# A two-layer diffusion trunk: the last output pair of layer 0 in another product order, and a conditioning block moved beside the last projection

## The chip, the core and the metric

The kernel runs on one core of a Trainium2 chip. The metric is the device time of one execution in microseconds (us). Three runs of the kernel before took 2236.32, 2233.32 and 2235.29 us; the median is 2235.29.

## The reference

One inference step of a trunk with two layers, width 2048, for 640 tokens: 128 context tokens and 512 latent tokens. All data are float32. A layer is

```python
h = rms_norm(x) * (1 + scale) + shift      # scale, shift, gate from silu(cond) @ ada_w + ada_b
y = mixer(h @ w_in, ...)                   # layer 0: banded attention and a short convolution
                                           # layer 1: differential attention (C) and dense attention (D)
x = x + gate * (y @ w_out)
```

`cond` differs between context and latent tokens, so each channel has two values (two "columns" c) of scale, shift and gate. Layer 1's attention also reads cached keys and values. Outputs are x after layer 1 and the new keys and values.

## The kernel before

**Layout.** Channels lie on the 128 partitions and the 640 tokens on the free axis; x, h and y are 16 tiles of 128x640, numbered k or n. A product of float32 is taken as three matmuls of a hi and a lo part: hi times hi, hi times lo, lo times hi. For that each operand is split: ScalarE (ACT) writes the hi part and VectorE (DVE) subtracts it (lines 329 and 330, function `split`; for weights the tiles are `wh` and `wl`, for activations both are called `h`). A matmul is 128x128 by 128x320, that is one half of the tokens: `HV[0]` is the first half, `HV[1]` the second. The time of the kernel is the PE's stream of these matmuls.

**Stages.** Even input projection, even mixer, output projection of layer 0 (`project_out(0)`), norm of its result, odd input projection ("front", `project`), attention of layer 1 with the rest of the odd columns beside it (`run_tiles`), output projection of layer 1 (`project_out(1)`).

**An output projection** makes three (layer 1: two) leading tiles, then single tiles, then pairs of output tiles. A pair (`run_pairs`) is done with seven products in the manner of Strassen, in the order M1, M5, M6, M2, M7, M3, M4; each product accumulates in one pair of PSUM banks `pq`, and DVE adds it to the residual `xr` (line 1292). M2 completes the first half of the pair's first tile, M7 the second half of its second tile, M3 the second half of its first and M4 the first half of its second (`done`).

**Norm of x1.** After the last pair of layer 0 (tiles 14 and 15), `norm_half` (line 1554) makes the norm of one half of the tokens: the square of the last tile on ACT (1557), sums over the channels as matmuls with a vector of ones (1565), mean and power on DVE and GpSimd (1567 to 1570), a transpose of the result r to a row that all partitions hold (1574), and its copy `rbc` by ACT (1577). `h1_maker` (1593) then makes h of row k: x1 times a scale times rbc on DVE (1611), the shift on ACT (1613), then the split. The x1 tiles come back from memory (`x1_back`), six of them beside the last products (`x1_tail`).

**Conditioning.** scale, shift and gate come in blocks of 512 columns of `ada_w`. For some blocks the product is made on DVE (`ada_rows`, lines 210 to 214): for each of 16 row blocks kt of the weights one load of 256 KB into a tile `adaw`, issued on GpSimd's queue (219), and two DVE instructions of 128x512 that add weight times silu(cond) to a tile `adaS` in PSUM. Block (1, 11) holds layer 1's gates of the output tiles 12 to 15. It runs in the attention stage as `fill1`, a generator from which the loop of `run_tiles` takes steps at the rate `FILL1`; its sums lie in a PSUM buffer of the pool "twice", which the attention scores share.

**Order.** Each engine works in its program order. The order in which the build writes the instructions is set by generators: `prep` (work for the next steps), `attn` (attention and other work beside the projections), `fill` (conditioning). `advance` takes steps from them at fixed places between matmuls, and a `yield` in a generator moves what stands behind it to the next such place. A scheduling pass of the build then orders instructions near one another by their operands. Loads of weights go out on SyncE's queue, stores and the loads of `adaw` on GpSimd's.

**First dense keys.** `keys_first` (1905) splits the first keys of the dense attention; its cached keys `ctxk` are loaded at the start of the attention stage (748) and transposed on PE (757).

The names that the change touches: `run_pairs` (575), `project` and `project_out` (1306, 1350), `x1_last` and `norm_half` (1544, 1554), `h1_maker` (1593), `fill1` (1879), `keys_first` (1905), `score_place` (84).

Of the kernel before, what the change touches and what calls it, by code (L numbers as in the profile page):

```python
# [20 lines left out]
P = 128  # L21
# [29 lines left out]
FILL0_FROM = 6  # L51
FILL1 = 1.15


@with_exitstack
def trunk_kernel(ctx: ExitStack, tc: tile.TileContext, I: dict, O: dict):
# [517 lines left out]

    def run_pairs(cols, w_ap, mov, room, used, begin, done, tail, fill=None, rests=lambda p, name: 0.0):

# [729 lines left out]

    def project(w, cols, n0, maker, job, begin, done, tail, n_lead=3, flip=0, fill=None, rests=lambda p, name: 0.0, **kw):

# [14 lines left out]
        for n in range(n_lead, n0):  # L1323
# [18 lines left out]
            if g is not None:  # L1342
# [3 lines left out]
                  {"B11": half_of(0, 0), "T1": half_of(0, 1), "B21": half_of(8, 0), "B22": half_of(8, 1),  # L1346
                   "T2": form_of(0), "T3": form_of(1), "T4": form_of(2)}, room, used, begin, done, tail, fill, rests)
        drain(prep)

    def project_out(l, maker, finish, last, tail, **kw):  # L1350
# [3 lines left out]
        def job(n):  # L1354
            def f(pp):
                if (l, n) not in loaded:
                    res_load(l, n)
                for i in range(2):
                    res_sum(l, n, pp[i], CS[:1] if i == 0 else CS[1:])
                yield  # L1360
                finish(n)
            return f

        def later(n):
            yield
            finish(n)
# [177 lines left out]
    def x1_last(t, h):  # L1544
        n, sl = KT - 2 + t, HV[h][1]
        if t == h:
            squares(n, sl)
            return
        nc.gpsimd.dma_start(xdram[n], st["xr", n])
        prep.append(norm_half(n, h))  # L1550
        if not h:
            drain(prep)


    def norm_half(n, h):
        sl = HV[h][1]
        A.activation(st["sq"][:, sl], st["xr", n][:, sl], AF.Square)
        yield
# [4 lines left out]
        for i, s in enumerate((st["acc"], st["sq"])):  # L1563
            for b, o in enumerate(starts):
                PE.matmul(tot[:, 4 * i + b:4 * i + b + 1], s[:, o:o + P], ones[:, 0:1], start=True, stop=True)
            if i == 0:
                V.tensor_scalar(ss, tot[:, 0:3], 1.0 / D, EPS, ALU.mult, ALU.add)
            else:
                V.scalar_tensor_tensor(out=ss, in0=tot[:, 4:7], scalar=1.0 / D, in1=ss, op0=ALU.mult, op1=ALU.add)
        G.tensor_tensor(r, ss, half[:, 0:3], op=ALU.pow)  # L1570
# [4 lines left out]
        if h:  # L1575
            st["rbc"] = xr_tile("rbc")
        A.copy(st["rbc"][:, sl], rt[:, 0:HALF])

    x1 = [None] * KT
    BACK = (0, 1, 2, 3, 8, 9, 10, 11, 4, 5, 6, 7, 12, 13)  # L1580
# [9 lines left out]

    project_out(0, y0_maker, x1_done, x1_last, x1_tail, early=early, flip=1)

    def h1_maker(k, hv):
        if k == 0 and hv[0][0]:
            for g in range(3):
# [3 lines left out]
            for i in (14, 15):  # L1599
                x1[i] = st["xr", i]  # L1600
        if k == 12:
            attn.append(forms(hdram))
        if len(hv) == 2 or hv[0][0]:
            new_h(k)
            st["ht", k] = big(f"T{4 + k % 4}")[:, 0:NT]
        t = st["ht", k]
        hi, lo = hs[k]
        toks = TOKS if len(hv) == 2 else (((0, slice(0, HALF), 0, 0),), CS[1:])[hv[0][0]]
        toks = [(x[-3], x[-1]) if len(x) == 4 else x for x in toks]
        for sl, c in toks:  # L1610
            V.scalar_tensor_tensor(out=t[:, sl], in0=x1[k][:, sl], scalar=gsc[1][:, k, c:c + 1],
                                   in1=st["rbc"][:, sl], op0=ALU.mult, op1=ALU.mult)
            A.activation(t[:, sl], t[:, sl], AF.Identity, bias=mod[1][:, k, c:c + 1])
# [258 lines left out]
    st["sets"], st["rp"] = 2, 3  # L1872
    place2, fold2 = (lambda t=t, n=n: pools["cur"].tile([P, NT], F32, tag=t, name="adaw", bufs=n) for t, n in (("x2", 1), ("kk", 2)))

    def scores_twice():
        st["once"] = True
        return pools["twice", "at"]

    fill1 = ada_in_psum([(1, 11)], scores_twice, place2, 1, (fold2, place2), "x2", 1)

# [23 lines left out]
    gated.clear()  # L1904
    def keys_first():
        key_split("k0", *first)
        yield
# [69 lines left out]
    jobs += [(OD["cg"] + i * P, last_gate(i)) for i in (4, 5)]  # L1977
    run_tiles(jobs, I["od_w_in"][0], None, fill1, FILL1, steps=lambda i: 3.3 if i < 5 else 1.85 if i < 13 else 2.6,
              single=lambda i: 0 if i else 2, fill_from=20)
    drain(prep)  # L1980
# [3 lines left out]
    def y1_maker(k):  # L1984
        if k in (6, 7):

            for _ in fill1:
                pass
            drain(attn)
# [40 lines left out]
    def rows_half(n, bs, late):  # L2030
# [4 lines left out]
        for i, b in enumerate(bs):  # L2035
# [62 lines left out]
```

## Time and profile before

| | |
|---|---|
| three runs, median | 2235.29 us (2233.32 to 2236.32) |
| the profiled execution's own time | 2233.99 us |
| its span | 2232.2 us |
| PE busy | 2200.3 us (99%) |
| DVE, ACT, POOL busy | 1745.4, 1137.0, 264.0 us |
| granted TensorE clock, mean | 0.998 |
| output projection of layer 0 ends, odd projection begins | about 1084 to 1091 us |
| odd front | to 1594 us |
| attention with the rest of the odd columns | 1594 to 2012 us |
| output projection of layer 1 | 2012 to 2228 us |

Times in the trace are counted from the start of the span; the profiled execution's own time holds 1.8 us more. Engines are PE (matmul), DVE (VectorE), ACT (ScalarE), POOL (GpSimd) and SP (SyncE). A row of the timeline has start, duration, engine, line of the kernel, operation, and "output<-inputs" by the program's names; in brackets stands how long the engine was idle before it and what ended that. The rows of waits give the sum in us, the number of waits and the longest. The rows of windows give, for a stretch, its length and each engine's busy time with the number of instructions, then the granted clock, the busy share of the DMA engines and GB/s. A matmul's duration (0.31 us) is longer than the distance to the next one, since matmuls are pipelined.

### The profile page before, as it was taken

The numbers are of one execution on the slowest core, as the hardware profiler recorded it, in microseconds if no ns is written. First come the engines' busy times: TensorE is split into PE (matmuls) and PEld (weight loads), VectorE is DVE, ScalarE is ACT, GpSimd is POOL, SyncE is SP. The second block draws the span as 40 slices with busy tenths as digits, with TensorE's granted clock in tenths as the row PEclk, the third lists the DMA queues.
The fourth block names the chain that finished last, engine by engine and source line by source line (L and its number), as shares of the span: only waits on it lengthen the run. The fifth ranks groups of instructions, "written<-read, shape, count | busy, mean of one in ns | idle before, by whom it ended". The sixth has DMA issues, their size and how long they took to land.

```text
span 2232.2 us, 41154 instructions
## 1 busy us (share of the span) xinstructions
PE 2200.3 (99%) x15516; PEld 2125.5 (95%) x15516; DVE 1745.4 (78%) x3047; ACT 1137.0 (51%) x2445; POOL 264.0 (12%) x421
## 2 busy tenths in 40 slices
PE   7999999999999999999999999999999999999999
PEld 5889999999999999999999999999999999999999
DVE  5659898989788977877788878978567687677665
ACT  4335453535334445444654466555578756664343
POOL 3221001000100100000101112211011111111010
PEclk9999999999999999999999999999999999999999
DMA  9985556565454435844675434545532343347541
GB/s 355 341 291 180 168 167 208 181 195 164 146 160 120 146 99 183 249 135 126 226 238 158 148 93 123 175 137 162 170 98 86 96 134 116 102 160 232 162 133 42
DMA packets 380375, 368.47 MB, mean 165 GB/s; under 512 B 18946, under 2 KB 326624, under 8 KB 379664
## 3 DMA queue, kind: packets, MB, share of 16 engines
q1 hardware_dynamic: 357248, 284.78, 42.0%
q0 software_dynamic: 22064, 78.83, 10.1%
q8 instruction: 122, 2.00, 0.4%
q10 hardware_dynamic: 864, 2.23, 0.3%
q14 instruction: 77, 0.63, 0.1%
HBM read 312.41 MB, written 48.11 MB: 162 GB/s over the span
## 4 chain that ended last, share of the span: by engine, by line
PE 90%; DMA 5%; DVE 2%; issue 1%; ACT 1%; POOL 1%; SPq 0%; DVEq 0%; POOLq 0%; ACTq 0%
PE pq L668 13%; PE pq L670 13%; PE pq L669 13%; PE pa L365 6%; PE pa L366 6%; PE pa L367 5%; PE pb L365 5%; PE pb L367 5%; PE pb L366 5%; PE T L908 2%; PE S L920 1%; PE S L922 1%; PE S L921 1%; PE T L698 1%; PE T L196 1%
## 5 line engine op out<-in xcount | busy, mean ns | idle before, releaser
L329 ACT ACTIVATE wh<-raw 128x512 fp32r<-128x512 f32 (+1 forms) x352 | 210.5, 600 | 315.6 <-PE pb L366 188.1
L668 PE MATMUL pq<-h,wh 128*128 128x320 f32 x1152 | 358.2, 311 | 0.0
L669 PE MATMUL pq<-h,wh 128*128 128x320 f32 x1152 | 355.9, 309 | 0.0
L670 PE MATMUL pq<-h,wl 128*128 128x320 f32 x1152 | 355.6, 309 | 0.0
L365 PE MATMUL pa<-h,wh 128*128 128x320 f32 x944 | 299.9, 318 | 0.5 <-DVE gg L1393 0.5
L365 PE MATMUL pb<-h,wh 128*128 128x320 f32 x944 | 296.1, 314 | 0.9 <-ACT h L329 0.9
L366 PE MATMUL pa<-h,wh 128*128 128x320 f32 x944 | 295.0, 313 | 0.4 <-DVE h L330 0.4
L367 PE MATMUL pb<-h,wl 128*128 128x320 f32 x944 | 293.9, 311 | 0.0
L367 PE MATMUL pa<-h,wl 128*128 128x320 f32 x944 | 293.5, 311 | 0.0
L366 PE MATMUL pb<-h,wh 128*128 128x320 f32 x944 | 292.9, 310 | 0.0
L330 DVE TENSOR_TENSOR wl<-raw,wh 128x512 fp32r<-128x512 f32 (+1 forms) x352 | 228.2, 649 | 74.4 <-ACT wh L329 66.7
L668 PE MATMUL pq<-T,wh 128*128 128x320 f32 x864 | 268.8, 311 | 0.0
L670 PE MATMUL pq<-T,wl 128*128 128x320 f32 x864 | 267.1, 309 | 0.0
L669 PE MATMUL pq<-T,wh 128*128 128x320 f32 x864 | 266.9, 309 | 0.0
L329 ACT ACTIVATE wh<-sx 128x512 fp32r<-128x512 f32 x216 | 135.8, 632 | 167.0 <-PE pq L669 110.2
L668 PEld LDWEIGHTS pq<-h,wh 128*128 128x128 f32 x1152 | 216.3, 188 | 1.6 <-issue 1.6
L669 PEld LDWEIGHTS pq<-h,wh 128*128 128x128 f32 x1152 | 216.4, 188 | 0.0
L670 PEld LDWEIGHTS pq<-h,wl 128*128 128x128 f32 x1152 | 216.3, 188 | 0.0
L283 DVE SCALAR_TENSOR_TENSOR acc<-adaw,sT,acc 128x1024 f32<-128x1024 f32 x150 | 189.3, 1276 | 1.3 <-DMA adaw<-in_ada_w 1.3
L365 PEld LDWEIGHTS pa<-h,wh 128*128 128x128 f32 x944 | 177.3, 188 | 12.9 <-issue 11.0
L330 DVE TENSOR_TENSOR wl<-sx,wh 128x512 fp32r<-128x512 f32 x216 | 147.7, 688 | 46.4 <-ACT wh L329 41.7
L366 PEld LDWEIGHTS pa<-h,wh 128*128 128x128 f32 x944 | 177.6, 188 | 4.7 <-issue 4.1
(416 smaller groups left out, 4985.3 us busy)
## 6 DMA issues: line engine op xcount, KB each, us to landing
adaw<-in_ada_w SPq DMA_DIRECT2D x80, 512.0 KB, 4.1
raw<-in_ev_w_in SPq DMA_DIRECT2D x130, 256.0 KB, 3.3
raw<-in_od_w_in SPq DMA_DIRECT2D x112, 256.0 KB, 3.2
w<-in_od_w_in SPq DMA_DIRECT2D x48, 512.0 KB, 4.5
ada<-in_ada_w SPq DMA_DIRECT2D x11, 2048.0 KB, 13.5
adaw<-in_ada_w POOLq DMA_DIRECT2D x75, 256.0 KB, 3.3
w<-in_ev_w_in SPq DMA_DIRECT2D x27, 512.0 KB, 3.8
adah<-in_ada_w SPq DMA_DIRECT2D x20, 512.0 KB, 9.1
```

The lines of the kernel that those rows point to most:

```text
L196: PE.matmul(acc[32 * g:32 * g + 32, 0:wd], sT[:, kt, :], w[:, kt % m, :], start=(i < 4), stop=(i >= KT - 4), tile_position=(0, 32 * g))
L283: V.scalar_tensor_tensor(out=acc[c], in0=w, scalar=sT[:, kt, c:c + 1], in1=acc[c], op0=ALU.mult, op1=ALU.add)
L329: A.activation(hi, x, AF.Copy)
L330: V.tensor_sub(lo, x, hi)
L365: PE.matmul(ps, wh[:, i, :], hi[:, sl], start=(j == js[0] if alone else (pos == 0 and j == 0)), stop=False)
L366: PE.matmul(ps, wh[:, i, :], lo[:, sl], start=False, stop=False)
L367: PE.matmul(ps, wl[:, i, :], hi[:, sl], start=False, stop=(j == js[1] - 1 if alone else (pos == 3 and j == 3)))
L668: PE.matmul(ps, wh[:, j, :], hi, start=(first and h == 0 and j == 0), stop=False, skip_group_check=True)
L669: PE.matmul(ps, wh[:, j, :], lo, start=False, stop=False, skip_group_check=True)
L670: PE.matmul(ps, wl[:, j, :], hi, start=False, stop=(final and h == 1 and j == 3), skip_group_check=True)
L698: PE.transpose(t[:, i * P:(i + 1) * P], src(b), ident)
L908: PE.transpose(t[:, i * P:(i + 1) * P], p, ident)
```

## The change

1. The last pair of layer 0 runs its products in the order M1, M5, M6, M7, M3, M2, M4 (`closing`). With that both second halves (M7, M3) are complete two products before the end. The norm of the second half is given to `prep` beside M2 and M4, the norm of the first half to `attn`, beside the first odd matmuls. `norm_half` takes the row sum of the earlier squares first and the last square behind it, and for the second half it makes h of rows 0 and 1 at once.
2. `h1_maker` multiplies x1 with rbc in one DVE instruction a row and gives the scale to ACT, which applies it with the shift.
3. `keys_first` begins with one more `yield`.
4. Block (1, 11) is taken from attention (`fill1`, `FILL1`, `st["once"]` go) and runs in `project_out(1)` as `fill2`: from single tile 4 on a step per quarter, then in the first pairs, and what is left of it before tile 12's pair begins. Its sums take the score buffer `pS`, its weights one tile `adaw`, later in turn with a third of `tables`. Score tiles of attention now always alternate between two buffers.
5. In layer 1 the residual tiles have four buffers in place of five, and the store of a tile stands one step later.

```diff
-    def run_pairs(..., fill=None, rests=lambda p, name: 0.0):
+    def run_pairs(..., fill=None, rests=lambda p, name: 0.0, closing=None):
...
-        seq = [(p, n) for p in range(len(cols)) for n in MOV]
+        seq = [(p, n) for p in range(len(cols)) for n in (closing if closing and p == len(cols) - 1 else MOV)]
...
     def score_place():
-        if ("twice", "at") not in pools or st.get("once"):
+        if ("twice", "at") not in pools:
...
-        st["xr", n] = pools["cur"].tile([P, NT], F32, tag="xr", name="xr", bufs=5)
+        st["xr", n] = pools["cur"].tile([P, NT], F32, tag="xr", name="xr", bufs=4 if l else 5)
...
                     advance(attn, 1 if len(hv) == 2 else 2)
+                    if n >= fill_at:
+                        next(fill, None)
...
         def begin(p):
             for t in range(2):
                 res_load(l, n0 + 2 * p + t)
+            if l and n0 + 2 * p >= 12:
+                for _ in kw.get("fill") or ():
+                    pass
...
     def x1_last(t, h):
         n, sl = KT - 2 + t, HV[h][1]
-        if t == h:
+        if not h:
+            nc.gpsimd.dma_start(xdram[n], st["xr", n])
+        if h and t:
             squares(n, sl)
-            return
-        nc.gpsimd.dma_start(xdram[n], st["xr", n])
-        prep.append(norm_half(n, h))
-        if not h:
-            drain(prep)
+        elif h:
+            prep.append(norm_half(n, h))
+        elif t:
+            attn.append(norm_half(n, h))
...
+        if not h:
+            squares(n - 1, sl)
+        columns(0, st["acc"])
+        V.tensor_scalar(ss, tot[:, 0:3], 1.0 / D, EPS, ALU.mult, ALU.add)
+        A.activation(st["sq"][:, sl], st["xr", n][:, sl], AF.Square)
+        yield
+        columns(1, st["sq"])
...
         A.copy(st["rbc"][:, sl], rt[:, 0:HALF])
+        if h:
+            for k in range(2):
+                st["ht", k] = xr_tile("ht")
+                h1_maker(k, HV[1:])
...
-        for i in {"M7": range(0, 4), "M3": range(4, 6)}.get(name, ()):
+        for i in {"M7": range(0, 3), "M3": range(3, 6)}.get(name, ()):
...
-        for sl, c in toks:
-            V.scalar_tensor_tensor(out=t[:, sl], in0=x1[k][:, sl], scalar=gsc[1][:, k, c:c + 1],
-                                   in1=st["rbc"][:, sl], op0=ALU.mult, op1=ALU.mult)
-            A.activation(t[:, sl], t[:, sl], AF.Identity, bias=mod[1][:, k, c:c + 1])
+        V.tensor_mul(t[:, sl], x1[k][:, sl], st["rbc"][:, sl])
+        for part, c in toks:
+            A.activation(t[:, part], t[:, part], AF.Identity, scale=gsc[1][:, k, c:c + 1], bias=mod[1][:, k, c:c + 1])
...
+    project_out(0, y0_maker, x1_done, x1_last, x1_tail, early=early, flip=1,
+                closing=("M1", "M5", "M6", "M7", "M3", "M2", "M4"))
...
-    fill1 = ada_in_psum([(1, 11)], scores_twice, place2, 1, (fold2, place2), "x2", 1)
+    fill2 = ada_in_psum([(1, 11)], lambda: pS, place2, 1, (fold2, lambda: tables[:, 2 * 512:3 * 512]), "adaw", 1)
...
     def keys_first():
+        yield
         key_split("k0", *first)
...
+    def fin_rests(p, name):
+        if p == 0 and name == "M1":
+            st["wide"] = [fold2, tables[:, 2 * 512:3 * 512]]
+        return float(name in ("M6", "M2", "M3", "M4"))
...
     project_out(1, y1_maker, rows_out, rows_last, lambda name: None, n_lead=2, order=(0, 2, 3, 1), led=last_pool,
-                lead_pp=(0, 2))
+                lead_pp=(0, 2), fill=fill2, fill_at=4, rests=fin_rests)
```

Lines of the kernel after are lower by one up to about line 1300 and higher by 14 to 31 behind that.

**PE at the border of the layers.** Of before, from the end of M4 (`pq<-T`) over the transposes of r and the column sums (`ones`) to the first odd matmuls (`pb<-h`):

```order
L669 MATMUL pq<-T_10983,wh 128x320
L670 MATMUL pq<-T_10983,wl 128x320
L1574 MATMUL T<-ident,r_12776 128x128 x2
L1574 MATMUL T<-ident,r_12776 128x64
L1565 MATMUL T<-ones,acc 128x1 x3
L1565 MATMUL T<-ones,sq 128x1 x3
L1574 MATMUL T<-ident,r_12809 128x128 x2
L1574 MATMUL T<-ident,r_12809 128x64
L365 MATMUL pb<-h_12858,wh 128x320 x2
L365 MATMUL Sp<-h_12858,wh 128x320
```

Of after, the same end of M4 and what follows:

```order
L668 MATMUL pq<-T_10983,wh 128x320
L669 MATMUL pq<-T_10983,wl 128x320
L1574 MATMUL T<-ones,acc 128x1 x3
L364 MATMUL pb<-h_12779,wh 128x320 x2
L365 MATMUL pb<-h_12779,wh 128x320
L366 MATMUL pb<-h_12779,wl 128x320
L365 MATMUL pb<-h_12779,wh 128x320
L366 MATMUL pb<-h_12779,wl 128x320
L364 MATMUL Sp<-h_12779,wh 128x320
L365 MATMUL Sp<-h_12779,wh 128x320
L364 MATMUL pb<-h_12786,wh 128x320 x2
L1574 MATMUL T<-ones,sq 128x1 x3
```

The transposes and sums no longer stand together: the row of r for the second half (`T<-ident,r_12729`) is now ahead of M4, and behind M4 stand only three column sums before odd matmuls of the second halves begin. The second sums of the first half follow after ten of them, its transposes after six more, and 20 second-half matmuls stand behind those before the first `pa` of a first half.

**PE at the first dense keys.** Of before, in the leading tiles of the attention stage (`Sp<-h`: the product of a lead; one `h` name for each row k):

```order
L365 MATMUL Sp<-h_13135,wh 128x320
L366 MATMUL Sp<-h_13135,wh 128x320
L367 MATMUL Sp<-h_13135,wl 128x320
L757 MATMUL T<-ident,ctxk 128x128 x2
L365 MATMUL Sp<-h_13144,wh 128x320
L366 MATMUL Sp<-h_13144,wh 128x320
L367 MATMUL Sp<-h_13144,wl 128x320
```

Of after:

```order
L364 MATMUL Sp<-h_13133,wh 128x320
L365 MATMUL Sp<-h_13133,wh 128x320
L366 MATMUL Sp<-h_13133,wl 128x320
L364 MATMUL Sp<-h_13141,wh 128x320
L365 MATMUL Sp<-h_13141,wh 128x320
L366 MATMUL Sp<-h_13141,wl 128x320
L756 MATMUL T<-ident,ctxk 128x128 x2
L364 MATMUL Sp<-h_12995,wh 128x320
```

The two transposes of `ctxk` stand behind two more rows of k, that is behind six more matmuls.

**DVE in the final projection.** Of before, from the last single tile's residual to the second product of the first pair (`wl`: lo parts of weights; lines 610 and 619: sums of weights for a product):

```order
L1292 SCALAR_TENSOR_TENSOR xr<-pb,hgt_137,xr 128x192
L1292 SCALAR_TENSOR_TENSOR xr<-pb,hgt_137,xr 128x128
L330 TENSOR_TENSOR wl<-w_25317,wh 128x512 x2
L330 TENSOR_TENSOR wl<-sx,wh 128x512
L1292 SCALAR_TENSOR_TENSOR xr<-pa,hgt_137,xr 128x320
L330 TENSOR_TENSOR wl<-sx,wh 128x512
L610 TENSOR_TENSOR sx<-sx,w_25317 128x1024
L330 TENSOR_TENSOR wl<-sx,wh 128x512 x2
L619 TENSOR_TENSOR sx<-w_25325,sx 128x1024
L330 TENSOR_TENSOR wl<-w_25325,wh 128x512 x2
```

Of after, at the same place:

```order
L1291 SCALAR_TENSOR_TENSOR xr<-pb,hgt_137,xr 128x192
L1291 SCALAR_TENSOR_TENSOR xr<-pb,hgt_137,xr 128x128
L213 SCALAR_TENSOR_TENSOR adaS<-adaw,sT,adaS 128x512
L329 TENSOR_TENSOR wl<-w_25242,wh 128x512
L213 SCALAR_TENSOR_TENSOR adaS<-tables,sT,adaS 128x512 x2
L329 TENSOR_TENSOR wl<-w_25242,wh 128x512
L213 SCALAR_TENSOR_TENSOR adaS<-adaw,sT,adaS 128x512
L329 TENSOR_TENSOR wl<-sx,wh 128x512
L213 SCALAR_TENSOR_TENSOR adaS<-adaw,sT,adaS 128x512
L1291 SCALAR_TENSOR_TENSOR xr<-pa,hgt_137,xr 128x320
L329 TENSOR_TENSOR wl<-sx,wh 128x512
L213 SCALAR_TENSOR_TENSOR adaS<-tables,sT,adaS 128x512
```

Behind the residual, each lo part now has two rows of the conditioning block (`adaS`) around it, on weights that come in turn in `adaw` and in `tables`.

More of the change, by code (lines that the diff above doesn't have):

```diff
@@ L573, in trunk_kernel, with run_pairs @@
     GROUP = {"M1": "M1", "M6": "M1", "M7": "M1", "M4": "M1", "M5": "M5", "M3": "M5", "M2": "M2"}
-    def run_pairs(cols, w_ap, mov, room, used, begin, done, tail, fill=None, rests=lambda p, name: 0.0):
+    def run_pairs(cols, w_ap, mov, room, used, begin, done, tail, fill=None, rests=lambda p, name: 0.0, closing=None):
         ap = pools["cur"]
@@ L1305, in form_of, with project @@
         return lambda j: (T[j][:, 0, i * HALF:(i + 1) * HALF], T[j][:, 1, i * HALF:(i + 1) * HALF])
-    def project(w, cols, n0, maker, job, begin, done, tail, n_lead=3, flip=0, fill=None, rests=lambda p, name: 0.0, **kw):
+    def project(w, cols, n0, maker, job, begin, done, tail, n_lead=3, flip=0, fill=None, rests=lambda p, name: 0.0,
+                closing=None, fill_at=KT, **kw):
         go_on = run_tiles([(cols[n], job(n)) for n in range(n_lead)], w, maker, **{"order": (0, 2, 1, 3), "flip": flip, **kw})
@@ L1346, in project @@
                   {"B11": half_of(0, 0), "T1": half_of(0, 1), "B21": half_of(8, 0), "B22": half_of(8, 1),
-                   "T2": form_of(0), "T3": form_of(1), "T4": form_of(2)}, room, used, begin, done, tail, fill, rests)
+                   "T2": form_of(0), "T3": form_of(1), "T4": form_of(2)}, room, used, begin, done, tail, fill, rests,
+                  closing)
         drain(prep)
@@ L1562, in norm_half, with columns @@
         r = small.tile([P, 3], F32, tag="r", name="r1")
-        for i, s in enumerate((st["acc"], st["sq"])):
+        def columns(i, x):
             for b, o in enumerate(starts):
[L1565 to L1569, printed above, removed]
+                PE.matmul(tot[:, 4 * i + b:4 * i + b + 1], x[:, o:o + P], ones[:, 0:1], start=True, stop=True)
+        if not h:
[3 more added lines that the diff above has]
+        A.activation(st["sq"][:, sl], st["xr", n][:, sl], AF.Square)
+        yield
+        columns(1, st["sq"])
+        V.scalar_tensor_tensor(out=ss, in0=tot[:, 4:7], scalar=1.0 / D, in1=ss, op0=ALU.mult, op1=ALU.add)
         G.tensor_tensor(r, ss, half[:, 0:3], op=ALU.pow)
@@ L1589, in x1_back @@
         nc.sync.dma_start(x1[k], xdram[k])
-    project_out(0, y0_maker, x1_done, x1_last, x1_tail, early=early, flip=1)
     def h1_maker(k, hv):
-        if k == 0 and hv[0][0]:
+        if len(hv) == 1 and k < 2 and hv[0][0] and k in made:
+            return
+        if k == 2 and hv[0][0]:
             for g in range(3):
@@ L1600, in h1_maker @@
                 x1[i] = st["xr", i]
+        if k == 0 and not hv[0][0]:
+            drain(attn)
         if k == 12:
@@ L1603, in h1_maker @@
         if len(hv) == 2 or hv[0][0]:
+            made.add(k)
             new_h(k)
-            st["ht", k] = big(f"T{4 + k % 4}")[:, 0:NT]
+            if k == 2:
+                st["T3"] = big("T3")
+            if k >= 2:
+                st["ht", k] = st["T3"][:, (k - 2) * NT:(k - 1) * NT] if k < 4 else big(f"T{4 + k % 4}")[:, 0:NT]
         t = st["ht", k]
@@ L1872, in trunk_kernel, with place2, fold2 @@
     st["sets"], st["rp"] = 2, 3
[L1873 to L1877, printed above, removed]
-    fill1 = ada_in_psum([(1, 11)], scores_twice, place2, 1, (fold2, place2), "x2", 1)
+    def place2():
+        if not st.get("wide"):
+            return pools["cur"].tile([P, NT], F32, tag="adaw", name="adaw", bufs=1)
+        st["wide"].reverse()
+        return st["wide"][0]() if callable(st["wide"][0]) else st["wide"][0]
+    def fold2():
+        return pools["cur"].tile([P, NT], F32, tag="adaw", name="adaw", bufs=1)
+    fill2 = ada_in_psum([(1, 11)], lambda: pS, place2, 1, (fold2, lambda: tables[:, 2 * 512:3 * 512]), "adaw", 1)
     def key_load(j, tag, bufs):
@@ L1977, in trunk_kernel @@
     jobs += [(OD["cg"] + i * P, last_gate(i)) for i in (4, 5)]
-    run_tiles(jobs, I["od_w_in"][0], None, fill1, FILL1, steps=lambda i: 3.3 if i < 5 else 1.85 if i < 13 else 2.6,
-              single=lambda i: 0 if i else 2, fill_from=20)
+    run_tiles(jobs, I["od_w_in"][0], None, steps=lambda i: 3.3 if i < 5 else 1.85 if i < 13 else 2.6,
+              single=lambda i: 0 if i else 2)
     drain(prep)
```

9 lines of the change are left out of this document (4 added, 5 removed).

## The prediction

> **What bounds the kernel now.** I read the totals first, then the chain that ended last, then the waits of PE summed by what they waited for, and only then single rows at the places where the change acts.
>
> ```profile
> span 2232.2 us, 41154 instructions
> PE 2200.3 (99%) x15516; PEld 2125.5 (95%) x15516; DVE 1745.4 (78%) x3047; ACT 1137.0 (51%) x2445; POOL 264.0 (12%) x421
> PE 90%; DMA 5%; DVE 2%; issue 1%; ACT 1%; POOL 1%; SPq 0%; DVEq 0%; POOLq 0%; ACTq 0%
> ```
>
> PE is busy for 2200.3 of 2232.2 us. The change adds and removes no matmul, so it can only win back PE's waits and slow stretches, or add some. This is what PE waited for behind the start-up (from 40 us on):
>
> ```profile
> PE T L1704 <- DVE on L1699: 1.7, 3, 0.7
> PE T L1574 <- POOL r L1570: 1.6, 2, 1.2
> PE T L757 <- DMA ctxk<-in_cache_d_k: 1.4, 1, 1.4
> PE T L908 <- DVE p L1667: 1.3, 3, 0.6
> PE Sp L365 <- ACT p L889: 1.0, 1, 1.0
> PE pb L365 <- ACT h L329: 0.9, 1, 0.9
> PE T L834 <- DVE ptl L330: 0.8, 3, 0.3
> ...
> PE pa L366 <- DVE h L330: 0.4, 1, 0.4
> ```
>
> The whole list is about 15 us long, so a gain above that is impossible unless a slow stretch goes too. There is one, at the border of the two layers.
>
> **The border of the layers (product order, norm, scale on ScalarE).** PE's rows from the last matmul of product M4 to the first odd matmul, then two odd matmuls one after the other, then the granted clock:
>
> ```profile
> 1083.54 0.30 PE L670 MATMUL pq<-T,wl 128*128 128x320 f32 x1
> 1084.22 0.88 PE L1574 MATMUL T<-ident,r 128*128 128x128 f32 x6 [0.38 <-POOL r L1570]
> 1084.93 0.78 PE L1565 MATMUL T<-ones,acc 128*128 128x1 f32 x6
> 1086.06 0.80 PE L1565 MATMUL T<-ones,sq 128*128 128x1 f32 x6 [0.35 <-ACT sq L1557]
> 1088.10 1.54 PE L1574 MATMUL T<-ident,r 128*128 128x128 f32 x6 [1.24 <-POOL r L1570]
> 1090.53 0.90 PE L365 MATMUL pb<-h,wh 128*128 128x320 f32 x2 [0.88 <-ACT h L329]
> ...
> 1093.10 0.47 PE L366 MATMUL pb<-h,wh 128*128 128x320 f32 x1
> 1093.37 0.47 PE L367 MATMUL pb<-h,wl 128*128 128x320 f32 x1
> ```
> ```profile
> 1083.80:1087.90 4.10, 2.34 (x19) 2.16 (x18) 2.70 (x9) 2.36 (x6) 1.70 (x3) 1.00 0.94 358
> 1087.90:1094.70 6.80, 5.71 (x22) 5.53 (x22) 5.24 (x14) 5.25 (x15) 0.74 (x2) 0.50 0.76 262
> ```
>
> The number 0.50 in the second row is the granted clock. In that stretch 128x320 matmuls start 0.27 us apart (1093.10 to 1093.37), where this kernel otherwise starts them 0.147 us apart (582 matmuls of this and smaller sizes in 84.00 us, in a row quoted below). The loss: from the end of the last slot of M4 (1083.54 + 0.15 = 1083.69) to 1090.53 are 6.84 us; some 15 slow matmuls up to 1094.70 lose 15 x 0.12 = 1.8 us; of these 8.6 us, about 2.0 are work that must be done anyway (two transposes of r at 0.71, the distance of 1084.22 and 1084.93, and two sets of column sums at 0.3). So 6.6 us are lost.
>
> After the change the norm of the second half of the tokens runs beside products M2 and M4, and its h for rows 0 and 1 are ready when M4 ends; the odd projection begins with second halves, and the norm of the first half runs beside them. The chain of that norm is the one of before, whose durations the trace has:
>
> ```profile
> 1087.15 0.90 POOL L1570 TENSOR_TENSOR r<-ss,half 128x3 f32<-128x3 f32 x1 [1.83 <-DVE ss L1569]
> ```
> ```profile
> 1089.68 0.42 ACT L1577 COPY rbc<-T 128x320 f32<-128x320 f32 x1 [1.55 <-PE T L1574]
> 1090.01 0.47 ACT L329 ACTIVATE h<-T 128x320 fp32r<-128x320 f32 x1
> 1090.38 0.73 ACT L1613 ACTIVATE T<-T,mod 128x128 f32<-128x128 f32 x2
> ```
>
> M4 now ends near 1084.75 (the same work, plus a third of a microsecond for a wait on the row sum in M2). The residual of the last tile takes 0.55 us on DVE, its square 0.47 on ACT, the sums 0.16 on DVE, the power 0.90 on POOL. With what stands queued between them on DVE and ACT (the second halves of rows 2 and 3), r is there near 1088.9, while PE reaches its transpose, in program order, after 16 matmuls, near 1088.3: a wait of 0.6 us. Then 20 more second-half matmuls (3 us) cover the copy of rbc (0.42) and the first halves of rows 0 to 3, of which each needs a scale of 0.73 and a hi part of 0.47 on ACT: 1.2 us a row, while PE consumes a row's first half in 9 matmuls, 1.3 us. The six early loads of x1 go out on SP with products M7 and M3 as before, of which M7 now comes one product sooner; they are there when M4 ends either way. So ACT just keeps pace, with up to 1 us of waits. What is left is 0.3 + 0.6 + some 0.7 = 1.6 us; **saving 6.6 - 1.6 = 5.0 us**. Bounds: 6.5 if nothing waits, 3 if the first halves come 1 us late at each of two rows. Here PE never rests for long, so I take the full clock.
>
> A rule weighed: the rows show no wait of PE above 1.24 us in the stretch, yet the clock halved for 6.8 us. The Trainium skill, "TensorE: Matmul & The Clock Gate", Part 1: The HAM clock gate (the "warmup" mystery), has the clock fall after an idle window of about 3.4 us and return after as long a busy one. The trace agrees on the size (6.8 us are two such windows), not on the word idle: the stretch before held small matmuls between its waits. By the letter of the rule the border of after, with waits of 0.6 us, keeps the full clock, and the sum is the one below; if a few waits suffice, as the rows of before show, rival 1 below decides.
>
> The scale of h moves from DVE (STT of 0.34 to 0.75 us, two or three a row) into the ACT instruction that adds the bias, and DVE does one multiplication a row. DVE's wait at 1115 us for an odd row's lo part (0.4 us in the list above) falls away, since DVE wins some 0.2 us for each row: **-0.3 us** (0 to -0.4; if ACT, which has as many instructions as before, became late instead, +0.4).
>
> **First dense keys split later.** Six matmuls of 0.147 us are now ahead of the transposes of ctxk, which wait for a DMA:
>
> ```profile
> 1597.90 0.31 PE L367 MATMUL Sp<-h,wl 128*128 128x320 f32 x1
> 1599.64 0.41 PE L757 MATMUL T<-ident,ctxk 128*128 128x128 f32 x2 [1.44 <-DMA ctxk<-in_cache_d_k]
> ```
>
> 1.44 - 6 x 0.147 = 0.55 us remain: **-0.9 us**. The load stands where it stood in SP's queue, and nothing else is moved past it; PE's next wait behind it is later by nothing, since the keys are first used far behind. Bounds 0 and -1.4.
>
> **The conditioning block leaves attention.** PE, DVE and the ada instructions in attention:
>
> ```profile
> 1605.00:1757.00 152.00, 151.94 (x1072) 141.23 (x1071) 101.17 (x189) 113.27 (x250) 15.22 (x15) 1.00 0.33 103
> 1757.00:1860.00 103.00, 100.55 (x706) 94.70 (x705) 84.08 (x158) 66.80 (x155) 20.11 (x33) 1.00 0.43 130
> 1860.00:1980.00 120.00, 118.34 (x823) 111.62 (x822) 81.33 (x160) 76.27 (x190) 17.18 (x29) 1.00 0.39 122
> ```
> ```profile
> L214 DVE SCALAR_TENSOR_TENSOR adaS<-adaw,sT,adaS x30: 735/754/756, 1763.2 to 1858.9; 128x512 f32<-128x512 f32 x30
> ...
>   DMA adaw<-in_ada_w: 9.8, 10
> ```
>
> While the block ran (1757 to 1860) PE lost 2.45 us, in the 152 us ahead of it 0.06. DVE was busy for 84 us and stood still for 9.8 us more in front of a load, with the attention's own work queued behind. Those waits are the ones on DVE in the list (p, on, ptl). Without the block's 32 ada rows (30 of line 214 and two first ones of the same size, 32 x 0.754 = 24.1 us) most of them go, but part of the waits are of the same sort as those from 1860 to 1980, which come to 1.7 us without any ada row: **-1.5 us** (0 to -2.5).
>
> The block also held half of the score tiles' second buffer. With two buffers throughout, the first product of the final projection, which takes the buffer of the 79th score tile and not that of the last, no longer waits for the last softmax:
>
> ```profile
> 2010.63 0.45 ACT L889 ACTIVATE p<-S,nm,rq 128x128 f32<-128x128 f32 x1
> 2010.97 0.20 ACT L889 ACTIVATION_READ_ACCUMULATOR p<-S,nm,rq 128x1 f32 x1
> ```
>
> PE's row at 2011.22 waited 1.0 us for it: **-1.0 us** (0 if it waits for another thing that is as late).
>
> **The block lands beside the final projection.** Its 24.1 us of DVE now lie between about 2041 and 2125. The windows of that stretch, of its second half, and of a stretch of the front that runs ada rows beside the same sort of products:
>
> ```profile
> 2041.00:2125.00 84.00, 84.00 (x582) 83.96 (x582) 56.73 (x99) 33.39 (x60) 8.23 (x13) 1.00 0.62 191
> 2089.90:2110.26 20.36, 20.36 (x142) 20.35 (x141) 10.48 (x16) 7.91 (x15) 1.29 (x2) 1.00 0.46 137
> 1420.00:1450.00 30.00, 30.00 (x209) 29.99 (x207) 29.78 (x46) 15.02 (x32) 7.47 (x14) 1.00 0.68 214
> ```
>
> DVE goes from 56.7 to 80.8 of 84 us: full, but not over. In the densest piece, 2089.9 to 2110.3, 16 rows (12.1 us) meet 20.4 - 10.5 = 9.9 us of room, so DVE falls 2.2 us behind. What PE allows is the distance between a lo part's end on DVE and its first use:
>
> ```profile
> 2101.42 0.69 DVE L330 TENSOR_TENSOR wl<-sx,wh 128x512 fp32r<-128x512 f32 x1 [1.04 <-ACT wh L329]
> ```
> ```profile
> 2105.59 0.31 PE L670 MATMUL pq<-T,wl 128*128 128x320 f32 x1
> ```
>
> That is 3.5 us, the least that I found in the stretch; others have 3.6 to 4.7. 2.2 is below 3.5, and the front ran with DVE at 29.8 of 30 us without a PE wait. But DVE works in order: a load that isn't there stops everything behind it.
>
> ```profile
> adaw<-in_ada_w POOLq DMA_DIRECT2D x75, 256.0 KB, 3.3
> ```
>
> With two buffers one block lasts 3.3 (landing) + 0.5 (issue) + 1.5 (two rows) = 5.3 us a buffer, 2.65 us a block, and eight blocks 21 us: just the stretch. I take **+1.0 us** for spots where it doesn't fit; bounds 0 and +6 (between this and rival 3). That the residual tiles of this layer have four buffers in place of five costs nothing by this view: a pair lasts some 26 us here, and only the next pair's two are loaded ahead; if the store came late, their 4 us of loading would still lie ahead of the pair's end.
>
> **Sum**: -5.0 - 0.3 - 0.9 - 1.5 - 1.0 + 1.0 = -7.7 us, 0.34%. The profiled execution took 2233.99 us (span 2232.2), 1.3 below the median of the runs; it becomes 2226.3, and the median 2235.29 - 7.7 = **2227.6 us**.
>
> **Rivals.**
> 1. The border keeps its slow stretch. For it: two waits of around 0.6 us are still in the new border, and the clock fell with waits of 1.24 us. Against: between them PE has full-width matmuls. Then 1.8 us of slow matmuls and about 1.8 us of waits stay: the sum is -4.1, 2231.2 us. Chance 0.12.
> 2. DVE in the final projection comes 3.5 to 5 us too late once per pair: +5 in place of +1, sum -3.7, 2231.6 us. For it: no room is left there. Against: the front. Chance 0.13.
> 3. Slower: the loads of the block, queued on POOL behind the stores of the output tiles, land in 8 us and not in 3.3. Then a buffer lasts 8 + 0.5 + 1.5 = 10 us, a block 5 us, and the ten blocks from 2090 on take 50 us against 35 that they have; 15 us late less 3.5 of slack is +11.5 us, and in the single tiles, with one buffer, six blocks take 60 us in place of 48 between 2041 and 2089, some +8 more. The sum is about +11, 2246 us; it turns to slower from landings near 7 us. Against: the DMA share there is 0.46, and the same load took 3.3 us beside a share of 0.43 in attention. Chance 0.08.
> 4. The change doesn't do what it says: attention's waits are of softmax, not of the ada rows, and the final projection's first product waits on another thing. Then -2.5 is missing: -5.2, 2230.1 us. Chance 0.07.
>
> The forecast itself has 0.60, its own range 2223.5 to 2230.5.
>
> **How the numbers follow.** About 0.2%, 4.5 us, is what a measurement of this kernel can tell from no change; the bound of faster is at 2230.8. Forecast and rival 4 are faster (0.67; I leave 0.01 of it to the other side), 1 and 2 within (0.25, with that 0.01 and part of 3's milder end 0.26), 3 slower (0.08). The range leaves out 3 and the ends of the forecast: 2223 to 2236.
>
> **What the profile of after would show.** Right: no slice of granted clock 0.50 between 1080 and 1100; PE's rows from M4 to the first odd matmul apart by 0.15; the waits on r (L1570) below 0.7 us together; the ctxk wait near 0.55; nearly no PE wait from 1750 to 1850; none of 1.0 at the head of the final projection; DVE near 96% from 2035 to 2120 with PE waits on wl below 1 us together. Wrong: a clock of 0.50 at the border; DVE waiting for adaw by more than 5 us in the final projection, and PE's lo products waiting on wl there.

## The result and the profile after

The change makes the kernel 0.14% faster: the ratio of after to before is 0.9986, with a 95% interval of 0.998 to 0.9991 (medians 2234.31 and 2238.11 us of 22 runs each). The forecast was 0.34%, and a gain of more than 0.2% with a chance of 0.66. The profiled execution has a span of 2230.1 us, 2.1 under before. The profiled execution of before was one of its faster ones (2233.99 us against a median of 2238.11), so a difference read from single traces can be some us smaller than the ratio of the runs says.

Totals of after, and what PE waited for from 40 us on:

```profile
span 2230.1 us, 41120 instructions
PE 2198.8 (99%) x15516; PEld 2126.8 (95%) x15516; DVE 1740.5 (78%) x3031; ACT 1139.5 (51%) x2445; POOL 264.4 (12%) x421
```
```profile
PE pq L669 <- DVE wl L329: 3.1, 2, 2.7
PE T L697 <- DVE m L743: 2.0, 1, 2.0
PE pa L365 <- DVE h L329: 1.9, 1, 1.9
PE T L697 <- issue: 1.6, 1, 1.6
PE T L1731 <- DVE on L1726: 1.3, 2, 1.0
...
PE T L756 <- DMA ctxk<-in_cache_d_k: 0.5, 1, 0.5
PE T L1588 <- POOL r L1584: 0.4, 1, 0.4
```

The waits that the change aimed at are gone or small: r at the border is 0.4 us in place of 1.6, ctxk 0.5 in place of 1.4, and the wait for the last softmax at the head of the final projection is missing. In their place stand three that before did not have: 1.9 us for a lo part of h, 2.7 us for a lo part of a weight, and 1.6 us at an output transpose.

Both programs have 15516 matmuls, so the start of the n-th matmul can be compared between two traces, and a stage's gain or loss is what the difference does across it, counted from the first matmul on (negative: earlier than before). The stages are cut at matmuls 7500 (1058 us in before, ahead of the border), 8400 (1196), 11000 (1571), 11400 (1631), 12000 (1715), 14100 (2022), 15300 (2196). The table has all kernels that were run, the experiments included; each row is one profiled execution.

| us against before | up to the border | border | front | first keys | to 1715 | rest of attention | final projection |
|---|---|---|---|---|---|---|---|
| after | +0.6 | -1.0 | 0.0 | -1.0 | 0.0 | **-6.6** | **+6.2** |
| e1_ring | +5.2 | -4.4 | 0.0 | -1.0 | 0.0 | -6.5 | +10.9 |
| e2_block_back | +2.6 | -1.3 | +0.1 | -1.1 | +0.1 | +2.0 | 0.0 |
| e3_one_score | +1.0 | -1.2 | 0.0 | -1.0 | +0.1 | -3.1 | +7.5 |
| e5_one_load | +0.8 | +1.0 | +0.1 | -1.1 | 0.0 | -6.6 | +0.1 |
| f2_block_front | +0.4 | -4.4 | 0.0 | +34.4 | +0.2 | -6.2 | 0.0 |
| f3_ring_block_back | +1.1 | -4.4 | 0.0 | -0.9 | 0.0 | +1.0 | 0.0 |
| g4_ring_scale_dve | +0.5 | -4.5 | 0.0 | -1.0 | 0.0 | -6.3 | +7.3 |
| h1_front_fast | +0.5 | -4.4 | +1.3 | -1.1 | +0.3 | -5.8 | 0.0 |

The first column shows how far single executions differ where the programs do the same work: +0.4 to +5.2 us. Among kernels that do the same work there, the other columns are steady to some 0.3 us, apart from the rest of attention without the block (-6.6 to -5.8), the final projection where it stalls (6.2 to 10.9), the border with tiles that wait for stores (-1.3 to +1.0), and attention with the block in it (+1.0 and +2.0 where before is 0).

So the gain was there, -8.6 us from border to attention, and the final projection gave 6.2 of it back. A second loss lies inside the border's -1.0.

**The border.** DVE, POOL and PE in after, then the windows of the border and of the place behind it:

```profile
1099.74 0.68 DVE L329 TENSOR_TENSOR wl<-raw,wh 128x512 fp32r<-128x512 f32 x1
1102.37 0.82 DVE L1636 TENSOR_TENSOR T<-T,rbc 128x640 f32<-128x640 f32 x1 [1.95 <-issue]
1103.12 0.48 DVE L1274 TENSOR_TENSOR tables<-w 128x320 f32<-128x320 f32 x1
1103.52 0.82 DVE L329 TENSOR_TENSOR h<-T,h 128x640 fp32r<-128x640 f32 x1
```
```profile
1097.14 0.54 POOL L1641 DMA_DIRECT2D hd<-T  x1 [1.27 <-DVE h L329]
```
```profile
1104.39 0.42 PE L365 MATMUL pa<-h,wh 128*128 128x320 f32 x1 [1.92 <-DVE h L329]
```
```profile
1088.20:1095.00 6.80, 6.35 (x42) 5.66 (x42) 4.33 (x11) 4.91 (x12) 2.39 (x4) 1.00 1.04 365
...
1104.30:1108.60 4.30, 4.21 (x19) 4.21 (x20) 3.67 (x6) 2.50 (x5) 0.54 (x1) 0.63 0.98 325
```

The old slow stretch is gone: the granted clock from 1088.2 to 1095 is 1.00, with 42 matmuls where before had 22. But 10 us later DVE stands for 1.95 us in front of a multiplication of `h1_maker`. Behind it in order is the lo part that PE needs, and PE waits 1.92 us. Then the clock is at half speed for 3.4 us (0.63 over the window). The multiplication writes a tile from which an earlier row's h is still being stored (1097.14). The trace names no releaser for this wait ("issue"), though it names the store for a later one of the same line:

```profile
1119.95 0.82 DVE L1636 TENSOR_TENSOR T<-xr,rbc 128x640 f32<-128x640 f32 x1 [1.10 <-DMA hd<-T]
```

So the store is a suspicion here, which e1_ring tests.

**The final projection.** POOL, DVE and PE of after around the longest wait, then two windows, and the landing times of the loads into `adaw` in after (here) and in before (in attention):

```profile
2087.20 0.54 POOL L218 DMA_DIRECT2D tables<-in_ada_w  x1 [3.52 <-DVE adaS L213]
```
```profile
2088.85 0.68 DVE L329 TENSOR_TENSOR wl<-w,wh 128x512 fp32r<-128x512 f32 x1
2092.91 1.55 DVE L213 SCALAR_TENSOR_TENSOR adaS<-tables,sT,adaS 128x512 f32<-128x512 f32 x2 [3.38 <-DMA tables<-in_ada_w]
2094.37 0.69 DVE L329 TENSOR_TENSOR wl<-w,wh 128x512 fp32r<-128x512 f32 x1
```
```profile
2095.11 0.52 PE L669 MATMUL pq<-h,wl 128*128 128x320 f32 x1 [2.71 <-DVE wl L329]
2095.42 0.47 PE L667 MATMUL pq<-h,wh 128*128 128x320 f32 x1
```
```profile
2091.00:2095.00 4.00, 1.39 (x10) 1.13 (x8) 2.05 (x4) 0.00 (x0) 0.25 (x1) 1.00 0.13 47
2095.00:2098.80 3.80, 3.69 (x16) 3.65 (x17) 3.80 (x8) 0.00 (x0) 0.83 (x2) 0.55 0.30 84
```
```profile
DMA to landing us min/median/max: 2.8/4.4/5.6
```
```profile
DMA to landing us min/median/max: 2.9/3.1/3.7
```

The load is issued at 2087.20, as soon as its buffer is free, and lands 5.7 us later. DVE, in order, stands for 3.38 us; the next lo part is done at 2095.06 instead of near 2091.7, and PE waits 2.71 us. The clock then falls to 0.55 for the window. The wait of 1.57 us at 2078.9 has the same origin: DVE had stood for 2.57 us in front of a load into `adaw` (up to 2075.55), and the residual that PE transposes stood behind it. 1.57 + 2.71 + some 1.5 for about 13 slow matmuls are 5.8 of the 6.2 us.

### The profile page after: what moved, and what is told of

Same layout as the page of the kernel before. It is cut to its first block, busy times and chain, and to the rows that moved or that the text cites. A ratio compares the mean times of both kernels' runs of the same rounds, so it can differ in the third digit from the quotient of the medians.

```text
span 2230.1 us, 41120 instructions
## 1 busy us (share of the span) xinstructions
PE 2198.8 (99%) x15516; PEld 2126.8 (95%) x15516; DVE 1740.5 (78%) x3031; ACT 1139.5 (51%) x2445; POOL 264.4 (12%) x421
```

## The experiments

**e1_ring: h without the wait for a store.** Rows 4 to 15 use three slots of each of four tiles.

```diff
-                st["ht", k] = st["T3"][...] if k < 4 else big(f"T{4 + k % 4}")[:, 0:NT]
+                g = (0, 1, 0, 2)[k // 4]
+                if 8 <= k < 12:
+                    st["T", k % 4] = big(f"T{4 + k % 4}")
+                st["ht", k] = st["T3"][...] if k < 4 else st["T", k % 4][:, g * NT:(g + 1) * NT]
```

> The kernel after, but h of rows 4 to 15 is made in three slots of four tiles, so that no row waits until an earlier row's store from the same tile has landed. Theory S (the store holds DVE, which works in order, and behind it the ready lo part that PE waits for): PE's wait of 1.92 us at 1104 us and the half clock behind it (1105.4 to 1108.5) go, and every later matmul starts some 3.4 us earlier than in the kernel after; the span is near 2226.7 us. Rival L (the x1 rows come late from memory, or ACT with the scale is too slow): the wait stays within 0.5 us of 1.9.

Measured: ratio 0.9973 (0.9963 to 0.9983). PE's waits from 1080 to 1120 us:

```profile
PE T L1588 <- POOL r L1584: 0.4, 1, 0.4
PE pa L365 <- DVE h L329: 0.2, 1, 0.2
```

The wait is gone, and the border is -4.4 us in place of -1.0; it stays gone in the four other kernels with these slots and is there (1.67 to 1.92 us) in the four without. Theory S holds. The span came out at 2236.1, not 2226.7, so that part of the expectation missed: 5.2 us were lost before the border, and the final projection stalled for 10.9 us. The slots are used at neither place, and g4_ring_scale_dve, which has them too, lost 0.5 and 7.3 us there.

**e2_block_back: the block back in attention.** The edit takes back part 4 of the change (`fill1`, `FILL1`, `st["once"]` as before; no `fill` in the final projection).

> The kernel after with the conditioning block back in attention (parts 1, 2, 3 and 5 of the change alone). If the block's move costs what the trace of after shows, the final projection runs as before (216 us from 2012 on, 6.5 us less than after) and attention as before (5.5 to 6.5 us more than after): the span is that of after within 1 us, some 2230. If the move's gain and price do not simply add, the difference is above 1.5 us.

Measured: ratio 0.9986 (0.9976 to 0.9995), span 2234.6. The final projection is as before to 0.05 us, the rest of attention 8.6 us longer than in after. So the price is the 6.2 us that was read off, but what the block costs attention is more than the trace of after had said (8.6, with 2.0 above before). The spans differ by 4.5 us, of which 2.0 lie ahead of the border, where a difference within 1 us was expected; the runs' ratio is the same with and without the move.

**e3_one_score: one score buffer, no block.**

```diff
-        if ("twice", "at") not in pools:
+        if ("twice", "at") not in pools or st.get("once"):
...
+    def once():
+        st["once"] = True
+        while True:
+            yield
+
-    run_tiles(jobs, I["od_w_in"][0], None, steps=..., single=...)
+    run_tiles(jobs, I["od_w_in"][0], None, once(), 1.15, steps=..., single=..., fill_from=20)
```

> The kernel after, in which the attention scores use one PSUM buffer in place of two from the point where the block began before, without any conditioning rows there. Theory B (the gain in attention comes from the second score buffer): attention loses most of the 6.5 us won between 1757 and 2012 us, the span is 4 to 6 us longer than after. Rival D (the gain comes from the DVE rows and the waits for their loads, as the prediction had it): it loses at most 1.5 us.

Measured: ratio 0.9993 (0.9984 to 1.0002). Attention loses 3.5 of the 6.6 us: neither theory alone. The score buffer is worth some 3.5 us, the rows and their loads some 3.1 (more by e2_block_back and f3_ring_block_back, whose attention is 1.0 to 2.0 above before).

**e5_one_load: DVE rows without loads.**

```diff
             fetch = lambda kt: ada_in(place()[:, 0:512], l, cb, kt, nc.gpsimd)
+            if l == 1 and cb == 11:
+                one = fetch(0)
+                fetch = lambda kt: one
```

> The kernel after, in which the block loads its weights once and all 16 row blocks use that one load (this leaves out the other 15 loads, so the gates of output tiles 12 to 15 get other values); its 32 DVE rows stay. Theory W (DVE, in order, stands in front of loads that haven't landed): PE's waits of 1.57 us at 2078.9 and 2.71 us at 2095.1 and the half clock go, the final projection is 5 to 6.5 us shorter than in after. Rival C (DVE has no room for the rows): PE still waits for lo parts by 2 us or more between 2050 and 2120.

Measured: ratio 0.9945 (0.9927 to 0.9962). The window over the stretch with all 32 rows of the block:

```profile
2010.00:2125.00 115.00, 115.00 (x794) 114.50 (x794) 96.01 (x164) 45.98 (x83) 12.03 (x19) 1.00 0.65 203
```

PE has no gap, with DVE busy for 96 of 115 us and the rows even closer together than in after (here they end at 2098, there at 2120). Theory W holds, C falls: the rows cost nothing, the loads cost 6.1 us. The edit takes away the loads' traffic as well as the waits for them; that it is the waits is read from the rows of after above.

**f2_block_front: the block in the odd front.** Made on e1_ring.

```diff
-    fill1 = ada_in_psum([(1, cb) for cb in range(8, 11)], lambda: pS, place1, 2, (place1, place1), "xr", 5)
+    fill1 = ada_in_psum([(1, cb) for cb in range(8, 12)], lambda: pS, place1, 2, (place1, place1), "xr", 5)
...
-                lead_pp=(0, 2), fill=fill2, fill_at=4, rests=fin_rests)
+                lead_pp=(0, 2))
```

> The kernel with three slots for h (as in the run without the store wait), in which the conditioning block runs as a fourth one of the odd front, where its loads go out two ahead, and no longer beside the final projection. Theory W (in the final projection the loads cost 6 to 11 us, the rows themselves nothing where PE's operands are split early enough): final projection as before, attention as in the kernel after, border 4.4 us shorter, first keys 1.0: 2220 to 2222 us of span, near 12 us under before. Rival C (32 more rows on DVE cost PE the same anywhere): the front becomes 3 us or more longer than the 478 us that it took before and after.

Measured: ratio 1.0087 (1.0073 to 1.0101). The expected 2220 to 2222 us were missed by some 35 us. Attention, border and final projection came out as expected, but the front's steps weren't enough for a fourth block; what was left ran after its last matmul, with PE standing:

```profile
1621.78 1.55 PE L252 MATMUL T<-adaw,ones 128*32 128x256 f32 x8 [33.95 <-ACT adaw L237]
```

That is a fault of the rate in this kernel and tells nothing of C; the stretch up to 1571 us is as long as before.

**f3_ring_block_back: parts 1, 2, 3 and 5 without the store wait.** The edits of e1_ring and e2_block_back together.

> Three slots for h, the block back in attention, so parts 1, 2, 3 and 5 with the store wait taken away. If the parts add up: border -4.4, first keys -1.0, attention and final projection as before: 5 to 6 us under before. If the border's gain is eaten by attention (rows that come earlier meet other waits), under 3.

Measured: ratio 0.9962 (0.9948 to 0.9975), 8.5 us at 2240: more than the sum of its stages (-4.4 - 0.9 + 1.0 = -4.3 us in the one profiled execution), so the expectation of 5 to 6 us is met only at the edge of what the interval allows (5.6 to 11.6).

**g4_ring_scale_dve: the scale back on DVE.** Made on e1_ring.

```diff
-        V.tensor_mul(t[:, sl], x1[k][:, sl], st["rbc"][:, sl])
         for part, c in toks:
-            A.activation(t[:, part], t[:, part], AF.Identity, scale=gsc[1][:, k, c:c + 1], bias=mod[1][:, k, c:c + 1])
+            V.scalar_tensor_tensor(out=t[:, part], in0=x1[k][:, part], scalar=gsc[1][:, k, c:c + 1],
+                                   in1=st["rbc"][:, part], op0=ALU.mult, op1=ALU.mult)
+            A.activation(t[:, part], t[:, part], AF.Identity, bias=mod[1][:, k, c:c + 1])
```

> Three slots for h, but the scale of h back on DVE as before (part 2 undone). If part 2 is worth what the prediction said, the border is 0.3 us longer than with the scale on ACT and a wait of PE for an odd row's lo part is back between 1095 and 1120 us. If DVE was the tighter engine in the new border, it is 1.5 us or more longer. If ACT was, it is shorter.

Measured: ratio 0.9966 (0.9954 to 0.9978), border -4.5 us against -4.4 with the scale on ACT. Two waits of 0.3 us appear at 1093 and 1094 us (one for DVE, one for ACT), and r no longer makes PE wait 0.4: it comes out even. Part 2 is worth nothing that can be seen.

**h1_front_fast: the front's steps made faster.** f2_block_front with

```diff
-            return {"M6": 0.5, "M2": 0.5, "M4": 1.0}.get(name, 0.0)
-        return {"M6": 1.0, "M2": 1.0, "M3": 1.0, "M4": 0.5 if out is gate_out else 1.75}.get(name, 0.0)
+            return {"M6": 1.0, "M2": 1.0, "M4": 1.5}.get(name, 0.0)
+        return {"M6": 1.5, "M2": 1.5, "M3": 1.5, "M4": 1.0 if out is gate_out else 2.25}.get(name, 0.0)
```

> Three slots for h and the conditioning block as a fourth one of the odd front, now with some 1.4 times as many steps a product, so that its last fold is done before the front ends. Theory W: the front keeps its length (DVE has 85 us of room in its 478), the standstill of 34 us at the front's end is gone, attention keeps the 6.5 us that it won and the final projection runs as before: some 12 us under before, ratio near 0.9945. Rival C (DVE too full in the front for a fourth block): the front is 3 us or more longer, and the ratio is above 0.996.

Measured: ratio 0.9942 (0.9929 to 0.9956), the lowest of all kernels here. Its front (1116 to 1594 us) and its final projection:

```profile
1116.00:1594.00 478.00, 476.11 (x3293) 472.20 (x3292) 406.48 (x653) 260.12 (x599) 82.53 (x145) 1.00 0.52 159
2007.00:2120.00 113.00, 113.00 (x783) 112.94 (x782) 75.53 (x130) 44.23 (x78) 11.05 (x18) 1.00 0.66 198
```

The front pays 1.3 us, 1.2 of them one wait at the fold of a block (1391.8 us), and the final projection has no gap. So the fourth block finds room in the front at a fifth of what the loads cost beside the final projection. Two things differ there: the loads go out two ahead, and the DMA engines are less busy (0.52 with all four blocks, against 0.66 in the final projection with none). No run separates the two.

## Why the prediction was wrong

The forecast was -7.7 us; the stages of after, from the border on, give -2.4, and the ratio of the runs -3.1 (-4.5 to -2.0, at 2238). By its steps:

- **Border, forecast -5.0 (3 to 6.5): -1.0. This step failed.** The chain was right: the wait for r was 0.4 us (forecast 0.6), the first halves came in time, the clock stayed at 1.00, and with the store wait taken away the border gives -4.4 (e1_ring). The forecast followed rows 0 to 3 and stopped there, and so put the rows behind at nothing. It did not follow DVE's queue to the rows behind, which come earlier now and meet tiles whose stores haven't landed: 1.92 us, and half clock behind it, 3.4 in sum.
- **Scale on ACT, forecast -0.3: 0 within 0.3** (g4_ring_scale_dve). The PE wait at 1115 us did go in after, but it returned in e2, e3 and e5 with 1.1 to 1.9 us, all kernels without the extra slots: with the slots it is missing in all five. So that wait too goes with the tiles and their stores, more than with what DVE spends on scales.
- **First keys, forecast -0.9: -0.9 to -1.1** in all kernels in which that place can be read. Right.
- **Attention, forecast -1.5 - 1.0 = -2.5: -6.6.** The mechanism of the rows was right, but the sum took only PE's listed waits; and of the score buffer only the last wait was counted, while it is worth 3.5 us over the whole stage (e3_one_score). Rival 4 (no gain) is refuted. The gaps of PE account for only 2.2 of the 6.6 us. Most of the gain lies at the score matmuls of 128x384, which start 0.187 us apart on the mean in before and 0.178 in after (219 and 214 pairs): it looks like waits so short that they hide in a matmul's modelled duration, and that no list of waits shows. In e3_one_score, with one buffer and no rows, the distance is 0.187 again. Summed from start to start, with the listed waits, the distances that end at such a matmul are 4.3 us shorter in after than in before, and 0.5 in e3_one_score. The remaining 2.2 us of after are spread over other matmuls.
- **Final projection, forecast +1.0 (0 to +6): +6.2. This step failed too, and by more than the border.** "3.3 (landing) + 0.5 (issue) + 1.5 (two rows) = 5.3 us a buffer" used the median landing of all 75 loads of that kind in the kernel; here the median of the 15 loads into the two tiles was 4.2, and three took 5.6. (In attention, for which the prediction also says 3.3, it was 3.1.) Blocks then arrive later than DVE comes to them, and DVE in order hands the delay to the lo parts; DVE's waits for these loads come to 11.7 us, the sign of being wrong that the prediction named. The size is near that of rival 2, the mechanism near that of rival 3: the loads, not the fullness of DVE (e5_one_load), though none took the 8 us of rival 3. The slack of 3.5 us was right as a number but was spent by one wait of 3.38 us. And the forecast left out what a PE wait can cost beyond itself: 1.5 us of half clock.
- **Four residual buffers, forecast 0: 0.** e2_block_back and f3_ring_block_back have them, and their final projection is as before to 0.05 us.

The misses are +4.0 at the border, +0.3 for the scale, -4.1 in attention and +5.2 in the final projection: 5.4 in sum, from -7.7 to about -2.4. That any gain is left is luck as far as the forecast goes: without the 4.1 us that attention gave beyond it, the kernel would not have become faster.

## What to carry to other kernels

When work for an in-order engine is moved next to critical work, its busy share is not the price: look at what each of its instructions waits for, with the landing times of loads and stores at the new place, because one late transfer holds all that is queued behind. When a chain is made earlier, follow the same queue on to the first tile that is reused, since its release (here a store's landing) did not move along. Put such side work where its loads can be two ahead and the DMA engines have room, even if the engine looks fuller there.

## What was not expected of the hardware

The same wait of PE near 174 us, 1.98 us in nearly every run, was followed by a slow stretch in some executions and not in others. The windows behind it in after and in before:

```profile
174.08:177.50 3.42, 3.42 (x16) 3.42 (x17) 3.42 (x7) 1.63 (x4) 0.00 (x0) 0.58 0.55 155
```
```profile
174.21:177.60 3.39, 3.39 (x24) 3.39 (x25) 3.39 (x7) 1.63 (x4) 0.00 (x0) 1.00 0.59 161
```

16 matmuls against 24, clock 0.58 against 1.00: some 1.1 us by chance alone. Of the ten profiled executions six have a half-clock stretch there and four have none. A wait of 1.57 us was once followed by half clock (g4_ring_scale_dve, 2064.6 us) and once not (after, 2078.9).

The records of the granted clock say why. In each trace the half-clock stretches begin whole multiples of 3.413 us apart (in after 273, 290 and 39 times that between its four), and all but the one at the end of the program last one such length or several. So the clock is decided in windows of 3.413 us that run on their own time. Here are such windows: in g4_ring_scale_dve the one with the wait of 1.57 us, in after the two that share the other wait of 1.57 us, and in e1_ring the two that share a wait of 2.55 us (2101.0):

```profile
2062.92:2066.33 3.41, 1.53 (x10) 1.23 (x10) 3.38 (x8) 0.79 (x2) 0.00 (x0) 1.00 0.97 292
```
```profile
2074.79:2078.20 3.41, 2.50 (x18) 2.23 (x16) 2.62 (x4) 3.00 (x7) 0.47 (x1) 1.00 0.35 127
2078.20:2081.61 3.41, 2.76 (x19) 2.56 (x20) 3.41 (x10) 0.76 (x2) 0.07 (x1) 1.00 0.66 183
```
```profile
2096.41:2099.82 3.41, 2.07 (x15) 1.81 (x13) 0.95 (x2) 0.54 (x1) 0.00 (x0) 1.00 0.34 98
2099.82:2103.23 3.41, 1.73 (x10) 1.47 (x10) 3.41 (x6) 0.00 (x0) 0.57 (x2) 1.00 0.25 76
```

PE stood for 1.88 us of the first (3.41 less 1.53), and half clock began at its end; it stood for at most 1.7 us of the others, and the clock stayed at 1.00. The same holds for all ten traces between 40 us and the last 8 us. Each window with 1.88 us or more of idle PE was followed by half clock (12 of them, besides the standstill in f2_block_front), of three with 1.77 or 1.78 us one was, and of those with 1.69 us or less only three: two at the border of before, where PE's work is in part one-column sums and small transposes, and the one in which the standstill of f2_block_front ends. So about half a window of idle PE was enough here, and whether a wait of 1.6 to 3 us costs half clock depends on how the windows cut it. In the start-up, ahead of 40 us, windows with up to 2.02 us idle kept the full clock; why, these runs leave open.

This fits a window that runs on its own time, as the Trainium skill has it ("TensorE: Matmul & The Clock Gate", Part 1: The HAM clock gate (the "warmup" mystery)), but about half a window of idle time was enough for half clock here, not the whole idle window of about 3.4 us that the page states.
